# A four-layer decoder trunk on one core: attention steps only after column products, and useless products in the sequence of a score

## The chip, the cores and the metric

One core of a Trainium2 chip runs the whole kernel. The metric is the device time of one execution in microseconds, and the median of several executions. The engines are TensorE (matrix products; the profile calls its products PE and its weight loads PEld), VectorE (DVE), ScalarE (ACT), GpSimd (POOL) and SyncE (SP, which issues the DMAs here).

## What is computed

The reference is a trunk of four residual layers over 256 tokens of width 1024, in fp32. Layers 0 and 3 mix tokens by dilated attention, layer 1 by a short gated convolution, layer 2 by a conformer convolution, and each layer ends in a gated ConvFFN of width 2816:

```python
for i in range(DEPTH):
    a = rms_norm(h, mix_norm_pre[i])
    m = (dilated_attention_mixer, short_conv_mixer, conformer_conv_mixer)[i % 3](a, ...)
    h = h + rms_norm(m, mix_norm_post[i])
    f = conv_ffn(rms_norm(h, ffn_norm_pre[i]), ffn_w_in[i], ffn_w_conv[i], ffn_w_out[i])
    h = h + rms_norm(f, ffn_norm_post[i])
```

The attention has three groups of 16 heads of 64 columns with windows and dilations (128, 1), (512, 4), (2048, 16). Queries and keys get a partial rotary turn. The three groups of a head are joined by the softmax of their log-sum-exp, which comes to one softmax over all three groups' scores together.

## The kernel before, in words

**Products.** Activations lie with the 1024 features on the partitions (eight blocks of 128) and the 256 tokens along the free axis. A weight arrives by DMA as fp32 (`raw`), ScalarE casts it to a high part (`whi`, L192) and VectorE subtracts that for the low part (`wlo`, L198); the activations are split likewise. `mm3` (L280 to L282) multiplies high by high, high by low and low by high. A "column" (`column`) is 128 output features of 256 tokens: 8 blocks x 3 products = 24 products of 128x256. `Stream.pump` casts weight pieces ahead of use, at most ten pieces.

**Useless products.** At the start of the ConvFFN, the short convolution and the conformer, `spread_later` (L342) makes a function that a later column calls within its products: it spreads the normalizing factor over the partitions (L324), lets ScalarE copy it, and then calls `settle` (L333), whose products nobody reads. They use 64 rows each, the lower and the upper half of the rows in turn.

**Attention (L810).** Heads go in quads of four and pairs of two. For each quad `order` (L110) gives the blocks: a and b are the first and second pair's queries and keys for a group (`qk_block`, two columns: 48 products), v the quad's values for a group (`value`, L880, two halves of 24 products, L894 to L896). The order is "a0 a1 v0 a2 v1 b0 v2 b1 b2", in the last quad "a0 a1 v0 a2 v1 b0 b1 b2 v2". The output of a `qk_block` gets its rotary turn on VectorE in halves (`one`, `two_`, for group 0 also `parts`), which stand in the list `later` and are taken one by one by `fill`.

Between the products of these blocks a generator does the rest of an earlier pair's work, one step at each call of `step()` (L981). Its steps for a pair (`pair_work`, L955) are: what is left in `later` is issued; scores of the first 128 tokens for both heads (`scores`, L902, products at L913, 64 rows each, the two heads in turn: three products of 256 columns and two of 128) and their softmax (`soften`: mask add with minimum L920, exponential L922, L924, L925 on VectorE and ScalarE); an empty step; the same for the other 128 tokens; four turns (`turn`: four transposes L931 into one bank, two copies on ScalarE L933); the weighting of the values (`weigh`, L942, then a split on ScalarE and VectorE). The first pair waits for LAG calls of `step()`. What is left after the last block stands between the output products, in pieces of 12 products.

`step()` is called in `qk_block` after each of its two columns, in `value` between its halves (L887) and once after a value block (L1015). PSUM has banks by tag: four "A" (columns, values), three "B" (scores take two, a turn one, a weighting one), one "S". A tile's bank is used again when its last reader is done.

Of the kernel before, what the change touches and what calls it, by code (L numbers as in the profile page):

```python
# [10 lines left out]
F32 = mybir.dt.float32  # L11
# [5 lines left out]
P = 128  # L17
D = 1024
T = 256
# [17 lines left out]
SPLIT = 60  # L37
FIRST = 10
EVERY = 3
LAG = 8  # L40
NCST = 2 * P + ROT // 2

PCOLS = {}
# [185 lines left out]
def trunk_kernel(ctx: ExitStack, tc: tile.TileContext, xT, pos, params, consts, masks, w8, out):  # L229
    nc = tc.nc  # L230
# [30 lines left out]
    def act(dt=F32, tag="act", bufs=NACT, shape=(P, 2, T)):  # L261
        counter[0] += 1
        return ap.tile(list(shape), dt, tag=tag, name=f"{tag}{counter[0]}", bufs=bufs)
# [11 lines left out]
    def psum(tag="A"):  # L275
        counter[0] += 1
        return ps.tile([P, 512], F32, tag=tag, name=f"ps{tag}{counter[0]}", bufs={"A": 4, "B": 3, "S": 1}[tag])
# [12 lines left out]
    def scaled(out, a, s, b=0.0):  # L290
        nc.scalar.activation(out=out, in_=a, func=AF.Identity, scale=s, bias=b)  # L291
# [28 lines left out]
    def spread(r):  # L320

        rb = psum("S")[:, :T]
        for c in range(2):
            nc.tensor.matmul(rb[:, c * P:(c + 1) * P], lhsT=r[:, c:c + 1].to_broadcast([P, P]), rhs=ident,  # L324
                             start=True, stop=True)
        return rb
# [6 lines left out]
    def settle(x, os):  # L333


        for _ in range(2):
            for half, o in enumerate(os):
                rows = slice(half * DH, (half + 1) * DH)
                nc.tensor.matmul(o, lhsT=x[0].bitcast(F32)[rows, 0:P], rhs=x[1].bitcast(F32)[rows, 0:P], start=True,
                                 stop=True, skip_group_check=True)  # L340

    def spread_later(r, x, banks):  # L342

        rb = act()[:, 0, :]

        def fill():
            o = spread(r)
            nc.scalar.copy(out=rb, in_=o)
            settle(x, [b[:, 0:P] for b in banks])

        return rb, fill

# [457 lines left out]
    def attention(l, mg, rb):  # L810
# [49 lines left out]
        def fill():  # L860
            if later:
                later.pop(0)()
            else:
                st.pump(1)
# [15 lines left out]
        def value(quad, g, hook=None):  # L880
            ws = [st.take(2 * P) for _ in range(2)]
            o = psum("A")
            at = (1, 0) if l == 0 else (0, 2)
            for c in range(2):
                if c:
                    fill()
                    step()  # L887
                oc = o[:, c * T:(c + 1) * T]
                for k in range(KD):
                    if hook and (c, k) == at:  # L890
                        hook()
                    whi, wlo, n = ws[k // 4]
                    xh, xl = [x[:, c * P:(c + 1) * P] for x in xs[k]]
                    nc.tensor.matmul(oc, lhsT=xh, rhs=whi[:, k % 4, :], start=k == 0, stop=False)  # L894
                    nc.tensor.matmul(oc, lhsT=xh, rhs=wlo[:, k % 4, :], start=False, stop=False)  # L895
                    nc.tensor.matmul(oc, lhsT=xl, rhs=whi[:, k % 4, :], start=False, stop=k == KD - 1)  # L896
            v = act()
            for c in range(2):
                scaled(v[:, c, :], o[:, c * T:(c + 1) * T], rt[0][:, c:c + 1])
            vs[quad, g] = v  # L900
# [16 lines left out]
        def soften(o, c):  # L917
            s = act()[:].rearrange("p s t -> p (s t)")
            mn, sm, rl = tiny(1), tiny(1), tiny(1)
            nc.vector.tensor_tensor_reduce(out=s, in0=o, in1=msk[:, c, :], scale=1.0, scalar=3e38,  # L920
                                           op0=ALU.add, op1=ALU.min, accum_out=mn)
            nc.scalar.activation(out=s, in_=s, func=AF.Exp, scale=-1.0, bias=mn, accum_out=sm)  # L922
            fill()
            nc.vector.reciprocal(out=rl, in_=sm)  # L924
            nc.vector.tensor_scalar(out=s, in0=s, scalar1=rl, scalar2=None, op0=ALU.mult)  # L925
            return s

        def turn(s, pt, c):
            o = psum("B")
            for b in range(4):  # L930
                nc.tensor.transpose(o[:, b * P:(b + 1) * P], s[:, b * P:(b + 1) * P], ident)  # L931
            for b in range(2):
                nc.scalar.copy(out=pt[b][:, :, c * P:(c + 1) * P],  # L933
                               in_=o[:, b * T:(b + 1) * T].rearrange("p (b t) -> p b t", b=2))
# [20 lines left out]
        def pair_work(pair):  # L955
            while later:
                later.pop(0)()
            pts = [(act(), act()) for _ in range(2)]
            ss = []
            os = scores(pair, 0)  # L960
            ss += [soften(o, 0) for o in os]
            yield
            yield
            os = scores(pair, 1)
            ss += [soften(o, 1) for o in os]
            yield
            turn(ss[0], pts[0], 0)
            yield
            turn(ss[1], pts[1], 0)
            yield  # L970
            for hp in range(2):
                turn(ss[2 + hp], pts[hp], 1)
                yield
            while (pair // 2, 2) not in vs:
                yield True
            weigh(pair, pts)
            yield
# [3 lines left out]
        def step():  # L981
            if wait[0]:
                wait[0] -= 1
                return
            for w in list(work):
                try:
                    if not next(w):
                        return
                except StopIteration:
                    work.remove(w)  # L990
# [13 lines left out]
        for quad in range(NQ):  # L1004
            for what, g in order(quad):
                if what == "v":
                    while later and quad == NQ - 1 and g == 2:
                        later.pop(0)()
                    if waiting and l == 0:
                        value(quad, g, before)  # L1010
                    else:
                        value(quad, g, ropes if waiting else None)
                        waiting = []
                    st.pump(2)
                    step()  # L1015
                    fill()
                    fill()
                    continue
                pair = 2 * quad + (what == "b")
                if pair == 0 and g < 2:  # L1020
                    waiting.append((first[g][:], (0, g)))
                else:
                    qk_block((pair, g), ropes if waiting else None)
                    waiting = []
                if g == 2:
                    work.append(pair_work(pair))
                    if pair == 0:
                        wait[0] = LAG
        ws = [st.take() for _ in range(4)]
# [15 lines left out]
        for d in range(4, KD):  # L1045
            o = column(ys, psum("B")[:, :T])
# [171 lines left out]
```

## Time and profile before

| | us |
|---|---|
| median of three executions | 1566.38 |
| lowest, highest | 1560.3, 1568.5 |
| the profiled execution | 1566.16 |
| its span, first to last instruction | 1564.3 |
| TensorE products busy | 1538.2 (98%) |
| TensorE weight loads busy | 1501.4 (96%) |
| VectorE busy | 1243.2 (79%) |
| ScalarE busy | 925.8 (59%) |
| mean granted TensorE clock | 0.995 |

All rows come from the profiled execution. Busy time is the time in which an engine has an instruction under way; products overlap in their pipeline, so the spacing of their starts tells more than their durations (a 128x256 product is listed with about 0.28 us, and the next one starts after about 0.11 us). "Idle before" is the time that an engine stood still ahead of an instruction, and the name behind the arrow is what ended it.

### The profile page before, as it was taken

How to read it: one execution, taken by the hardware profiler on the slowest of the kernel's cores; microseconds unless marked ns; L12 is line 12 of the kernel's file. 1: busy time of each engine (PE TensorE's matmuls, PEld its weight loads, DVE VectorE, ACT ScalarE, POOL GpSimd, SP SyncE). 2: the span in 40 equal slices, each digit the busy share in tenths (PEclk: the TensorE clock that was granted, in tenths of full speed). 3: DMA queues.
4: the chain of work that ended last, by engine and by line, in shares of the span. 5: the costliest groups of instructions: out<-in, count | busy, mean ns of one | idle time of the engine just before them, and what ended most of it. 6: DMA issues, size and time to landing. Idle time of an engine off the chain costs nothing.

```text
span 1564.3 us, 31521 instructions
## 1 busy us (share of the span) xinstructions
PE 1538.2 (98%) x13194; PEld 1501.4 (96%) x13194; DVE 1243.2 (79%) x2177; ACT 925.8 (59%) x1623; POOL 17.9 (1%) x51
## 2 busy tenths in 40 slices
PE   6999999999999999999999999999999999999998
PEld 6999999999999999999999999999999999999997
DVE  4997877698886779888699588896888778588783
ACT  6564645575574566656576666566546446565562
POOL 4000000000000000000000000000000000000000
PEclk9999999999999999999999999999999999999999
DMA  5663433266552644655333136553544334245540
GB/s 218 216 213 139 162 141 130 81 218 223 195 202 103 219 162 167 238 197 201 115 135 108 55 135 244 191 186 135 216 162 164 133 136 163 107 156 222 190 162 28
DMA packets 36718, 256.94 MB, mean 164 GB/s; under 512 B 4320, under 2 KB 4448, under 8 KB 5984
## 3 DMA queue, kind: packets, MB, share of 16 engines
q1 hardware_dynamic: 36288, 254.93, 45.2%
q8 instruction: 103, 1.69, 0.4%
q14 instruction: 39, 0.32, 0.1%
q10 hardware_dynamic: 288, 0.01, 0.0%
HBM read 253.87 MB, written 1.05 MB: 163 GB/s over the span
## 4 chain that ended last, share of the span: by engine, by line
PE 93%; DVE 3%; ACT 1%; POOL 1%; issue 1%; DMA 1%; DVEq 0%; ACTq 0%; POOLq 0%
PE psA L537 17%; PE psB L280 10%; PE psB L282 10%; PE psB L281 10%; PE psA L280 7%; PE psA L281 7%; PE psA L282 7%; PE psA L894 3%; PE psA L895 3%; PE psA L896 3%; PE psB L731 2%; PE psB L942 2%; PE psB L913 2%; PE psA L453 2%; PE psB L931 2%; PE psA L448 2%
## 5 line engine op out<-in xcount | busy, mean ns | idle before, releaser
L198 DVE TENSOR_TENSOR wlo<-raw,whi 128x1024 fp32r<-128x1024 f32 x480 | 580.2, 1220 | 34.6 <-ACT whi L192 33.9
L192 ACT CAST whi<-raw 128x1024 fp32r<-128x1024 f32 x480 | 491.1, 1049 | 22.8 <-DMA raw<-in_w_dram 17.2
L282 PE MATMUL psB<-act,wlo 128*128 128x256 f32 x1392 | 385.6, 277 | 0.0
L280 PE MATMUL psB<-act,whi 128*128 128x256 f32 x1392 | 385.6, 277 | 0.0
L281 PE MATMUL psB<-act,whi 128*128 128x256 f32 x1392 | 385.6, 277 | 0.0
L280 PE MATMUL psA<-act,whi 128*128 128x256 f32 x1040 | 298.6, 287 | 8.0 <-ACT whi L192 7.1
L282 PE MATMUL psA<-act,wlo 128*128 128x256 f32 x1040 | 290.0, 279 | 0.5 <-DVE wlo L198 0.5
L281 PE MATMUL psA<-act,whi 128*128 128x256 f32 x1040 | 290.1, 279 | 0.2
L537 PE MATMUL psA<-act,whi 128*128 128x256 f32 x1536 | 265.1, 277 | 0.0
L282 PEld LDWEIGHTS psB<-act,wlo 128*128 128x128 f32 x1392 | 262.5, 189 | 0.0
L281 PEld LDWEIGHTS psB<-act,whi 128*128 128x128 f32 x1392 | 261.3, 188 | 0.0
L280 PEld LDWEIGHTS psB<-act,whi 128*128 128x128 f32 x1392 | 261.3, 188 | 0.0
L537 PEld LDWEIGHTS psA<-act,whi 128*128 128x128 f32 x1536 | 231.7, 188 | 0.0
L537 PE MATMUL psA<-act,wlo 128*128 128x256 f32 x768 | 212.9, 277 | 0.0
L280 PEld LDWEIGHTS psA<-act,whi 128*128 128x128 f32 x1040 | 197.0, 189 | 13.6 <-ACT whi L192 7.1
L282 PEld LDWEIGHTS psA<-act,wlo 128*128 128x128 f32 x1040 | 196.9, 189 | 0.8 <-DVE wlo L198 0.8
L281 PEld LDWEIGHTS psA<-act,whi 128*128 128x128 f32 x1040 | 196.9, 189 | 0.6 <-DVE act L285 0.5
L291 ACT ACTIVATE tmp<-act,par 128x256 f32<-128x256 f32 x176 | 80.2, 503 | 161.7 <-DVE act L285 161.7
L288 DVE SCALAR_TENSOR_TENSOR tmp<-act,par,tmp 128x255 f32<-128x255 f32 (+1 forms) x352 | 146.6, 479 | 19.7 <-ACT tmp L291 19.7
L537 PEld LDWEIGHTS psA<-act,wlo 128*128 128x128 f32 x768 | 144.9, 189 | 0.0
L285 DVE TENSOR_TENSOR act<-psB,act 128x512 f32<-128x512 f32 (+2 forms) x94 | 58.5, 625 | 82.2 <-PE psB L282 45.3
L922 ACT ACTIVATE act<-act,tiny 128x512 f32<-128x512 f32 x64 | 46.4, 725 | 110.3 <-DVE tiny L920 110.3
(126 smaller groups left out, 2189.1 us busy)
## 6 DMA issues: line engine op xcount, KB each, us to landing
raw<-in_w_dram SPq DMA_DIRECT2D x239, 1024.0 KB, 4.8
h<-in_xT_dram SPq DMA_DIRECT2D x4, 256.0 KB, 5.0
raw<-in_w_dram SPq DMA_DIRECT2D x2, 512.0 KB, 5.5
out_dram<-h SPq DMA_DIRECT2D x4, 256.0 KB, 2.0
msk<-in_masks_dram SPq DMA_DIRECT2D x1, 512.0 KB, 9.4
par<-in_params_dram SPq DMA_DIRECT2D x1, 484.0 KB, 10.1
cst<-in_consts_dram SPq DMA_DIRECT2D x1, 132.0 KB, 5.9
par<-in_params_dram ACTq DMA_DIRECT2D x1, 4.0 KB, 2.9
```

Of the source, the lines that this page charges most:

```text
L192: self.nc.scalar.copy(out=hi, in_=raw)
L198: self.nc.vector.tensor_tensor(out=lo, in0=raw, in1=hi.bitcast(F32), op=ALU.subtract)
L280: nc.tensor.matmul(o, lhsT=whi, rhs=x[0], start=first, stop=False)
L281: nc.tensor.matmul(o, lhsT=whi, rhs=x[1], start=False, stop=False)
L282: nc.tensor.matmul(o, lhsT=wlo, rhs=x[0], start=False, stop=last)
L285: nc.vector.tensor_tensor(out=out, in0=a, in1=b, op=op)
L288: nc.vector.scalar_tensor_tensor(out=out, in0=a, scalar=s, in1=b, op0=op0, op1=op1)
L291: nc.scalar.activation(out=out, in_=a, func=AF.Identity, scale=s, bias=b)
L537: nc.tensor.matmul(o, lhsT=a, rhs=b, start=first and i == 0, stop=last and i == 2, skip_group_check=True)
L894: nc.tensor.matmul(oc, lhsT=xh, rhs=whi[:, k % 4, :], start=k == 0, stop=False)
L895: nc.tensor.matmul(oc, lhsT=xh, rhs=wlo[:, k % 4, :], start=False, stop=False)
L896: nc.tensor.matmul(oc, lhsT=xl, rhs=whi[:, k % 4, :], start=False, stop=k == KD - 1)
```

## The change

It changes three things. `settle` issues five pairs of products instead of two, of 256, 256, 256, 128 and 128 columns instead of 128 and 128 (the second operand and the output are that wide). `value` no longer calls `step()` between its halves, and the block loop no longer calls it after a value block. In `pair_work` the empty step is gone, the four turns are taken two to a step, and LAG is 6 instead of 8.

```diff
-LAG = 8
+LAG = 6
...
     def settle(x, os):
 
 
-        for _ in range(2):
+        for n in (T, T, T, P, P):
             for half, o in enumerate(os):
                 rows = slice(half * DH, (half + 1) * DH)
-                nc.tensor.matmul(o, lhsT=x[0].bitcast(F32)[rows, 0:P], rhs=x[1].bitcast(F32)[rows, 0:P], start=True,
-                                 stop=True, skip_group_check=True)
+                nc.tensor.matmul(o[:, :n], lhsT=x[0].bitcast(F32)[rows, 0:P], rhs=x[1].bitcast(F32)[rows, 0:n],
+                                 start=True, stop=True, skip_group_check=True)
...
             o = spread(r)
             nc.scalar.copy(out=rb, in_=o)
-            settle(x, [b[:, 0:P] for b in banks])
+            settle(x, banks)
...
             for c in range(2):
                 if c:
                     fill()
-                    step()
                 oc = o[:, c * T:(c + 1) * T]
...
             os = scores(pair, 0)
             ss += [soften(o, 0) for o in os]
             yield
-            yield
             os = scores(pair, 1)
             ss += [soften(o, 1) for o in os]
             yield
-            turn(ss[0], pts[0], 0)
-            yield
-            turn(ss[1], pts[1], 0)
-            yield
-            for hp in range(2):
-                turn(ss[2 + hp], pts[hp], 1)
+            for c in range(2):
+                for hp in range(2):
+                    turn(ss[2 * c + hp], pts[hp], c)
                 yield
...
                     st.pump(2)
-                    step()
                     fill()
                     fill()
                     continue
```

## Rows read from the trace of the kernel before

**Rows 1.** Busy time of each engine in three stretches: attention of layer 0, two ConvFFN.

```profile
66.00:293.00 227.00, 225.34 (x2064) 216.03 (x2062) 178.13 (x318) 127.30 (x244) 0.00 (x0) 1.00 0.44 158
911.00:1084.00 173.00, 172.45 (x1508) 171.29 (x1505) 146.35 (x238) 110.21 (x175) 0.00 (x0) 1.00 0.56 201
1378.00:1551.00 173.00, 173.00 (x1472) 172.88 (x1472) 134.49 (x219) 100.02 (x162) 0.00 (x0) 1.00 0.46 165
```

The columns are the stretch, its length, then busy us of PE, PEld, DVE, ACT and POOL, the granted clock, the share of the DMA engines and GB/s.

**Rows 2.** TensorE's groups by line and shape: busy us, mean ns, idle before.

```profile
L895 PE MATMUL psA<-wlo,act 128*128 128x256 f32 x384 | 107.6, 280 | 0.0
...
L731 PE MATMUL psB<-act,tmp 128*128 128x256 f32 x156 | 34.2, 378 | 0.0
```

**Rows 3.** TensorE in order of time, ConvFFN of layers 2 and 3: start, length, instruction.

```profile
909.92 0.60 PE L324 MATMUL psS<-cst,tiny 128*128 128x128 f32 x4
910.45 0.71 PE L339 MATMUL psB<-act 64*128 64x128 f32 x8
...
1078.84 0.50 PE L306 MATMUL psS<-cst,tmp 128*128 128x1 f32 x4
...
1377.35 0.68 PE L324 MATMUL psS<-cst,tiny 128*128 128x128 f32 x4
1377.96 0.71 PE L339 MATMUL psB<-act 64*128 64x128 f32 x8
...
1552.91 0.50 PE L306 MATMUL psS<-cst,tmp 128*128 128x1 f32 x4
```

**Rows 4.** TensorE in order of time, layer 0's attention, around scores and a turn.

```profile
152.99 0.28 PE L896 MATMUL psA<-whi,act 128*128 128x256 f32 x1
153.11 0.28 PE L894 MATMUL psA<-whi,act 128*128 128x256 f32 x1
...
159.74 0.28 PE L282 MATMUL psA<-act,wlo 128*128 128x256 f32 x1
159.85 0.28 PE L280 MATMUL psA<-act,whi 128*128 128x256 f32 x1
...
162.12 0.28 PE L282 MATMUL psA<-act,wlo 128*128 128x256 f32 x1
162.24 0.60 PE L931 MATMUL psB<-cst,act 128*128 128x128 f32 x4
...
162.80 0.28 PE L895 MATMUL psA<-wlo,act 128*128 128x256 f32 x1
```

**Rows 5.** VectorE and TensorE in order of time at layer 3's first pair.

```profile
1132.35 3.49 DVE L198 TENSOR_TENSOR wlo<-raw,whi 128x1024 fp32r<-128x1024 f32 x3
...
1133.93 0.39 PE L913 MATMUL psB<-act 64*128 64x256 f32 x2
...
1135.76 0.74 DVE L843 STREAM_SHUFFLE act<-psA 128x512 f32<-128x512 f32 x1
...
1138.32 0.69 DVE L920 CUSTOM_DVE_ANT_0 act<-psB,msk 128x512 f32<-128x512 f32 x1
```

**Rows 6.** The same at layer 0's last pair, which stands among the output products.

```profile
263.48 0.39 PE L913 MATMUL psB<-act 64*128 64x256 f32 x2
...
264.58 0.69 DVE L920 CUSTOM_DVE_ANT_0 act<-psB,msk 128x512 f32<-128x512 f32 x1 [0.15 <-PE psB L913]
...
272.89 0.49 DVE L925 TENSOR_SCALAR act<-act,tiny 128x512 f32<-128x512 f32 x1
```

**Rows 7.** The same at a weighting of layer 0 and its split on VectorE.

```profile
118.64 1.96 PE L942 MATMUL psB<-act,act 128*64 128x256 f32 x24
...
121.77 0.42 DVE L285 TENSOR_TENSOR act<-psB,act 128x256 fp32r<-128x256 f32 x1
```

**Rows 8.** What TensorE waited for, whole span: us in total, times, longest.

```profile
PE psB L913 <- DVE act L285: 1.7, 2, 0.8
...
PE psA L280 <- ACT act L437: 0.9, 2, 0.5
```

**Rows 9.** A group of the page: busy us, mean ns, idle before.

```profile
L192 ACT CAST whi<-raw 128x1024 fp32r<-128x1024 f32 x480 | 491.1, 1049 | 22.8 <-DMA raw<-in_w_dram 17.2
```

## The prediction

> **What bounds the kernel now.** I read the table of busy time by stretch first. In the attention stretch of layer 0 TensorE is busy for 225.3 of 227 us and VectorE for 178.1; in the ConvFFN of layers 2 and 3 TensorE is busy for 172.5 and 173.0 of 173 us, all at a granted clock of 1.00, which is the 2.4 GHz level [rows 1]. So TensorE is the bound nearly everywhere: a product that is added costs its full length, and a wait that is added costs its full length as long as TensorE stands in it.
>
> The second view is TensorE's instructions in order of time. Products of one shape (128x256) start at two different spacings. After the second score products of layer 0's pair 3, column products start about 0.113 us apart (159.74, 159.85); after its first ones, where value products follow, 0.118 us (152.99, 153.11) [rows 4]. Rounded starts hide the exact values; over a whole ConvFFN they show. From the start of the useless products to the first product of the closing sum it takes 1078.84 - 910.45 = 168.39 us in layer 2, and 1552.91 - 1377.96 = 174.95 us in layer 3, for the same instructions [rows 3]. That is 6.56 us, about 4.4 ns for each of some 1,480 products, so a "fast" and a "slow" spacing last until something else than a plain stream comes. What differs ahead: in layer 3 the four spreading products take 0.68 us, 0.08 more than in layer 2 (0.60), so they stood a moment waiting for their operand [rows 3]. The useless products (`settle`) evidently set the spacing most of the time, and once did not.
>
> **Useless products: what is added.** Today a call is four 64-row fp32 products of 128 columns, two row halves side by side; they leave eight records and take 0.71 us [rows 3]; there are six calls (four ConvFFN, the short convolution, the conformer). The change keeps the two 128-column pairs at the end and puts three 256-column pairs ahead. The operands are still read as fp32, so each is recorded as two passes (the eight records show it), and six more passes of 256 columns run per call, halves side by side. A 256-column fp32 pass costs 34.2 / 156 = 0.219 us in the conformer [rows 2]. So 6 calls x 6 x 0.219 = **+7.9 us**. Could it be hidden? Nothing stands beside it: TensorE is busy for 99 to 100% of what follows [rows 1], and the copy of the spread factor is issued ahead of it, so VectorE and ScalarE start no earlier or later. The ends: +3.9, if a 64-row pass needed half of that, as a 128-column transpose (0.109) is about half of it [rows 4], and +7.9; I take 7.9, since the row has the same width and type.
>
> **Useless products: what they bring.** Where score products are followed by column products the spacing is fast, even after the pair whose score products waited 0.8 us in their midst [rows 8] (I looked through all of them; [rows 4] has one). If the longer call works like them, layer 3's ConvFFN comes down to 168.39: **-6.6 us**.
>
> The Trainium skill, page "TensorE: Matmul & The Clock Gate", section "Back-to-back issue gap", speaks against this: it gives the spacing of an isolated stream from width and clock alone (N/2.4 + 2.5, 109 ns at 256 columns), so what stood before could change nothing, and the -6.6 would be left out of the sum. The trace does not agree: neither spacing is 109 ns, and two stretches of equal work at the same clock differ by 6.56 us [rows 1, 3].
>
> **Turned tiles, two to a step.** A turn takes from the last product ahead of it (162.12) to the second behind it (162.80) 0.68 us [rows 4]; less two products (0.227) and four transposes of 0.109 (0.60 less one length of 0.27, over three), some 17 ns are the cost of going in and out. 32 such steps go away: **-0.5 us**.
>
> **Spacing in the attention stages.** Steps no longer fall into a value block, but one may still come right before it, and score or turned products followed by value products gave the slow spacing [rows 4]. By the new order six of twelve value blocks of a layer still follow a score or a turn. Even if all 1,152 value products (384 a line [rows 2]) went from slow to fast, it would be 1,152 x 4.4 ns = 5.1 us. I take 0, and -5 to +3 as ends.
>
> **Steps that come closer together: new waits.** Per layer, 44 slots are left instead of 68, a pair uses five instead of eight, and its empty slot is gone. Where no value block lies between, score 1 now comes one column (24 x 0.1133 = 2.7 us) behind score 0, and the first two turns one column behind that. Three things then gate TensorE: the three banks of tag B (score 1's second bank is score 0's first, free when its mask add is done; the second turn's bank is score 1's first), the softmax itself, and VectorE's queue ahead of it (weight differences, and the rotary halves that `pair_work` flushes). The last pair of layer 0 shows the softmax with nothing in its way: the score starts at 263.48, the first mask add at 264.58 (+1.1), the fourth tile is done at 273.38, so 2.2 us a tile [rows 6]. With a queue: in layer 3's first pair three weight differences (3.49 us, 1.14 each) and two rotary halves (2.56 us, 1.28 each) stand ahead, and the mask add comes 4.4 us after the score [rows 5].
>
> By pairs, from the start of score 0:
> - Pair 0 starts two columns later (+5.4 us for TensorE), and VectorE does the last difference, one half, two more differences and three flushed halves, ending 9.2 us after today's start: mask add at +3.8 to +4. Score 1 wants its bank at +3.7 and gets it at +4.7: 1.0 waited. The third mask add follows two tiles (4.4) and a difference (1.1): done at +10.2, where the second turn comes at +8.9: 1.3. The last tile (+13.9) is then in time. 2.2 us.
> - Pair 2: VectorE meets TensorE at the weighting, whose split ends 3.5 us after its start [rows 7]; a difference and two flushed halves later the mask add is at +2.6, the third one ends at +8.8 and the second turn wants it at +8.0: 0.8 us.
> - Pairs 1, 3: a value block lies between: 0. Pairs 4, 6: value blocks empty the rotary queue ahead of them, mask add at +1.1 to +1.5: 0.
> - Pair 5 needs the rotary halves that it flushes itself, and today already waits 0.8 us for them in each layer [rows 8]. Without the column that lay between, 2.0 us: 1.2 more.
> - Pair 7 stands among the output products, which come in 1.4 us pieces: the second turn comes 1.0 us ahead of its bank, the last tile (+9.9 [rows 6]) is 1.4 us late; the wait of 0.5 behind the last weighting [rows 8] is covered by two pieces: 1.9.
>
> 6.1 us a layer, **+12.2 us** for two. The ends: 0, if VectorE were as free as in [rows 6] and the pieces fell well, and some +20: ScalarE issues the copies of the first turns behind the last exponentials and perhaps behind a weight cast of 1.05 us [rows 9], which would delay the bank of the fourth turn by about 0.9 us in four pairs of a layer (+7). I take the sum without it, because in [rows 6]'s pair the copies came right behind the exponential.
>
> Queues: score 1's mask adds move ahead of a column's weight difference on VectorE, the turns' copies ahead of a cast on ScalarE; pieces are taken well ahead of use, so I cost that at nothing. SP's and POOL's queues have no step in them, and weight loads keep their order.
>
> **The sum** against the profiled execution (1566.16 us, a span of 1564.3; the median of the runs is 1566.38, 0.2 above): 1566.2 + 7.9 - 6.6 - 0.5 + 12.2 = **1579 us**. A measurement can tell some 0.5% from no change, 7.8 us here: faster is below 1558.5, slower above 1574.2.
>
> **Rivals.**
> - Not slower: the waits do not come. Place: second turn and score 1's bank in pairs 0 and 2. It decides if the first mask add comes within about 1.8 us of the score, as in [rows 6], also there. Then 1579 - 12.2 = 1567. For it: VectorE is idle for a fifth of the stage [rows 1]. Against: the 4.4 us of [rows 5].
> - The useless products do not do what they should: one ConvFFN stays slow, 1579 + 6.6 = 1586. For it: the last four passes are the same as today's, which failed once. Against: the score products' record.
>  By the Trainium skill's formula above, the -6.6 would likewise not come.
> - ScalarE's copies gate the fourth turn as well: 1579 + 7 = 1586, to 1593 with the rival before.
> - Faster: value products lose their slow spacing and no waits come: 1567 - 5 = 1562, still within 0.5%; below 1558.5 needs the 7.9 us to be cheaper too (the low end, 3.9).
>
> **How the numbers follow.** The sum 0.44 (own range 1572 to 1584), no waits 0.24, `settle` fails 0.14, copies 0.10, faster 0.08. The first case lies above 1574.2 for nine tenths, so slower is 0.40 + 0.14 + 0.10, less 0.01 for mixtures: 0.63; same 0.24 + 0.04 + 0.01 = 0.29; faster 0.08. For 8 in 10 the range goes from the no-wait case with some of its spacing gain, 1563, to both failures short of their sum, 1590.
>
> **What would show it.** Right: `settle` at about 2.0 us a call; all four ConvFFN at 168.4 plus 1.3; waits of TensorE's score and transpose lines on VectorE's mask add of some 12 us in all, mostly in pairs 0 and 7. Wrong: one ConvFFN at 176, waits under 4 us, or longer waits on ScalarE's copies than on VectorE.

## The result, and the profile after

The changed kernel takes **1611.62 us** (median of four executions, 1608.14 to 1614.70) where the kernel before takes 1566.86 beside it (four executions, 1560.30 to 1568.50): a ratio of 1.0306, with a 95% interval of 1.0276 to 1.0335. Slower was forecast; 1579 us and a range that ended at 1590 were not enough.

The profiled execution took 1614.70 us with a span of 1612.8, which is 48.5 us more than the span before. Line numbers have moved: the score products are L912, the mask add is L919, the scaling L924, the turn L930 and its copies L932.

First the page of the changed kernel: the span, the busy time of each engine, and the shares of the chain that ended last. The last line is that of the kernel before.

```profile
span 1612.8 us, 31675 instructions
...
PE 1565.2 (97%) x13266; PEld 1521.8 (94%) x13266; DVE 1244.1 (77%) x2177; ACT 925.3 (57%) x1623; POOL 18.2 (1%) x51
...
PE 80%; DVE 11%; ACT 4%; issue 2%; DMA 1%; POOL 1%; DVEq 0%; ACTq 0%; POOLq 0%
...
PE 93%; DVE 3%; ACT 1%; POOL 1%; issue 1%; DMA 1%; DVEq 0%; ACTq 0%; POOLq 0%
```

VectorE and ScalarE have the work that they had before (1243.2 and 925.8 us), yet VectorE now stands in 11% of the chain instead of 3%. It was not given work; it is now waited for. TensorE's busy time grew by 27 us, far more than the 7.9 us of added products: some of its products follow each other more slowly.

**Useless products and ConvFFN.** TensorE in order of time, the answers to [rows 3], in layer 0 and layer 2: the spreading, the useless products, and the first product of the closing sum. Columns are start, length and instruction.

```profile
328.36 0.60 PE L324 MATMUL psS<-cst,tiny 128*128 128x128 f32 x4
328.89 2.01 PE L339 MATMUL psB<-act 64*128 64x256 f32 x20
...
505.13 0.39 PE L306 MATMUL psS<-cst,tmp 128*128 128x1 f32 x3
...
945.61 0.60 PE L324 MATMUL psS<-cst,tiny 128*128 128x128 f32 x4
946.14 2.01 PE L339 MATMUL psB<-act 64*128 64x256 f32 x20
...
1115.81 0.39 PE L306 MATMUL psS<-cst,tmp 128*128 128x1 f32 x3
```

A call takes 2.01 us instead of 0.71: 1.30 more, as forecast. From its start to the closing sum it takes 505.13 - 328.89 = 176.24 us in layer 0 and 1115.81 - 946.14 = 169.67 in layer 2. Layer 1 is like layer 0 (176.24), layer 3 like layer 2 (169.69). Before it was 168.39 in layers 0 to 2 and 174.95 in layer 3 [rows 3]. So layer 3 did get the fast spacing that the prediction hoped for, but layers 0 and 1 lost it. The spreading took 0.60 us here in layers 0 and 2 alike, so no wait tells the two apart. What does is the column ahead of the spreading. I measured spacings as means over the products of a stretch, since the rounded starts hide them: where the products ahead came 113.4 ns apart, those behind the call came 117.5 to 117.8 ns apart (three times of three, layer 0 among them), and where they came 117.5 to 117.8 ns apart, those behind came 113.3 ns apart (three of three). **The new call turns the spacing over; the old one set it fast.**

With the short convolution (75.91 to 77.19) and the conformer (86.16 to 87.82), the stretches behind the six calls grew by 7.85 + 7.85 + 1.28 - 5.26 + 1.28 + 1.66 = 14.7 us, where the prediction had 7.9 - 6.6 = 1.3.

**Attention.** From the sum of the normalization ahead of the attention (in layer 3 that of layer 2's end) to that of the one behind it, layer 0 grew from 268.13 to 286.39 us and layer 3 from 280.76 to 297.74, together 35.3 us, where the prediction had 12.2 - 0.5 = 11.7. With 14.7 that is 50.0 us; the rest of the kernel got 1.5 us shorter, which I did not follow. What TensorE waited for, whole span, us in total, times and longest (the answer to [rows 8]):

```profile
PE psB L930 <- DVE tiny L919: 9.9, 8, 2.7
...
PE psB L912 <- DVE act L285: 6.2, 4, 2.1
...
PE psB L930 <- ACT act L932: 4.0, 8, 0.7
PE psB L930 <- DVE act L924: 2.0, 2, 1.0
PE psB L912 <- DVE tiny L919: 1.6, 3, 0.6
```

These five lines are 23.7 us. The same lines of before hold 1.9: 1.7 for L913 [rows 8], and this one for the turns:

```profile
PE psB L931 <- DVE tiny L920: 0.2, 1, 0.2
```

The longest wait is in pair 0 of layer 0. TensorE and VectorE there, in order of time, from the first scores on:

```profile
72.12 0.39 PE L912 MATMUL psB<-act 64*128 64x256 f32 x2
...
76.06 0.38 PE L912 MATMUL psB<-act 64*128 64x256 f32 x1
76.35 0.68 DVE L919 CUSTOM_DVE_ANT_0 act<-psB,msk 128x512 f32<-128x512 f32 x1
...
77.09 0.38 PE L912 MATMUL psB<-act 64*128 64x256 f32 x1 [0.65 <-DVE tiny L919]
...
80.92 0.60 PE L930 MATMUL psB<-cst,act 128*128 128x128 f32 x4
81.20 2.36 DVE L198 TENSOR_TENSOR wlo<-raw,whi 128x1024 fp32r<-128x1024 f32 x2
83.48 0.68 DVE L919 CUSTOM_DVE_ANT_0 act<-psB,msk 128x512 f32<-128x512 f32 x1
84.23 0.65 PE L930 MATMUL psB<-cst,act 128*128 128x128 f32 x4 [2.71 <-DVE tiny L919]
85.42 0.28 PE L280 MATMUL psA<-act,whi 128*128 128x256 f32 x1
85.53 0.35 PE L281 MATMUL psA<-act,whi 128*128 128x256 f32 x1
...
85.89 0.42 PE L280 MATMUL psA<-act,whi 128*128 128x256 f32 x1
86.11 0.41 PE L281 MATMUL psA<-act,whi 128*128 128x256 f32 x1
```

The first mask add comes 4.2 us after the score (76.35 - 72.12), so the second scores wait. The second turn could start at 81.4, but its bank holds the second half's first scores, whose mask add stands behind two weight differences on VectorE (2.36 us from 81.20) and comes at 83.48. Then a second loss begins that the prediction did not have. The column that follows starts its products 0.11 us apart at first (85.42, 85.53) and then 0.21 to 0.22 us apart (85.89, 86.11): TensorE's clock has gone down to the 1.2 GHz level after the wait of 2.71 us. Busy time by stretch shows the granted clock (the third number from the end; the columns are those of [rows 1]). A whole ConvFFN of this kernel has 1.00 there.

```profile
84.50:89.10 4.60, 4.60 (x29) 4.60 (x28) 4.45 (x9) 4.02 (x7) 0.00 (x0) 0.63 1.00 390
221.00:225.70 4.70, 4.70 (x30) 4.42 (x26) 2.63 (x9) 2.38 (x5) 0.00 (x0) 0.64 0.01 3
1322.00:1327.80 5.80, 5.80 (x30) 5.35 (x28) 3.48 (x9) 2.56 (x5) 0.00 (x0) 0.50 0.00 0
```

The second and third stretches stand behind waits of 2.14 us in pair 5 of layers 0 and 3. In all three TensorE is listed as busy all the time: a column at the lower level looks like work. From its first product to the next step such a column took 4.43, 4.54 and 5.42 us, where a column elsewhere in these stages takes 2.8 to 3.0: some 1.6, 1.6 and 2.5 us were lost.

### The profile page after: what moved, and what is told of

Read it like the earlier page. It is cut to its first block, busy times and chain, and to the rows that moved or that the text cites. A ratio compares the mean times of both kernels' runs of the same rounds, so it can differ in the third digit from the quotient of the medians.

```text
span 1612.8 us, 31675 instructions
## 1 busy us (share of the span) xinstructions
PE 1565.2 (97%) x13266; PEld 1521.8 (94%) x13266; DVE 1244.1 (77%) x2177; ACT 925.3 (57%) x1623; POOL 18.2 (1%) x51
## 4 chain that ended last, share of the span: by engine, by line
PE 80%; DVE 11%; ACT 4%; issue 2%; DMA 1%; POOL 1%; DVEq 0%; ACTq 0%; POOLq 0%
PE psA L537 16%; PE psB L282 10%; PE psB L280 10%; PE psB L281 10%; PE psA L280 4%; PE psA L282 4%; PE psA L281 4%; DVE wlo L198 3%; DVE act L285 3%; PE psA L893 2%; PE psA L894 2%; PE psA L895 2%; PE psB L731 2%; PE psB L941 2%; PE psA L453 2%
## 5 line engine op out<-in xcount | busy, mean ns | idle before, releaser
L282 PEld LDWEIGHTS psA<-act,wlo 128*128 128x128 f32 x1040 | 200.1, 192 | 0.8 <-DVE wlo L198 0.8
L288 DVE SCALAR_TENSOR_TENSOR tmp<-act,par,tmp 128x255 f32<-128x255 f32 (+1 forms) x352 | 146.6, 478 | 19.7 <-ACT tmp L291 19.7
L537 PEld LDWEIGHTS psA<-act,wlo 128*128 128x128 f32 x768 | 145.7, 190 | 0.0
```

The source lines that it names most:

```text
L282: nc.tensor.matmul(o, lhsT=wlo, rhs=x[0], start=False, stop=last)
L288: nc.vector.scalar_tensor_tensor(out=out, in0=a, scalar=s, in1=b, op0=op0, op1=op1)
L537: nc.tensor.matmul(o, lhsT=a, rhs=b, start=first and i == 0, stop=last and i == 2, skip_group_check=True)
```

## The experiments

Twelve runs were made, of eleven kernels. Each is set against the kernel before as it was timed beside that run. Theory A was, in short, that the new call turns the spacing over and that the steps cost waits because they stand too close together; each run says what the others were. Line numbers are those of each kernel.

### The new useless products alone

The kernel before with the change's `settle` and the wider banks, and nothing else:

```diff
-        for _ in range(2):
+        for n in (T, T, T, P, P):
...
-            settle(x, [b[:, 0:P] for b in banks])
+            settle(x, banks)
```

> The kernel before with the new useless products alone (five pairs, three of them 256 columns wide); the attention steps are as before. In the changed kernel each of the six calls left the other spacing than the one that the column ahead of it had: 113.4 became 117.8 ns three times, 117.5 to 117.8 became 113.3 three times. Theory A (the longer call turns the spacing over, whatever it was): the same here in all six calls, so the ConvFFN whose column ahead is fast take 176.2 us from the call to the closing sum, those whose column ahead is slow 169.7; with two to four slow ones the time is 1573 to 1594 us, at least 7 us over the kernel before. Rival B (the changed kernel's waits in the attention stages brought the slow ConvFFN, the call itself sets the fast spacing): all four at 169.7, time 1566 to 1570 us.

Measured: 1585.28 us (1575.05 to 1591.15, four executions) against 1560.72, ratio 1.0149 (1.0104 to 1.0195). In the profiled execution the four ConvFFN took 169.69, 176.24, 176.24 and 169.69 us from call to closing sum, and the spacing turned over behind all six calls (two from fast to slow, four from slow to fast). Attention kept its length. That is theory A; with the six calls of the changed kernel it makes twelve of twelve. The executions lie 16 us apart, which would follow if the columns ahead differ between them; only one was profiled.

### The steps alone

The change with the old `settle`: LAG, the two `step()` calls, the empty step and the turns as in the change's diff.

> The changed kernel with the old useless products (two pairs of 128 columns): the change of the steps alone. Theory A (the two attention stages lost 35 us to waits, to refilling after them and to stretches at half clock, whatever the useless products are): 1596 to 1604 us, TensorE's waits in score and transpose lines some 24 us in the profile, stretches with product starts 213 ns apart. Rival B (a good part of the attention's loss comes through the spacing that the useless products leave): under 1590 us.

Measured: 1594.83 us (1592.89 to 1598.18), ratio 1.0220 (1.0205 to 1.0235): 34.1 us more, just under theory A's range and over its rival's. All four ConvFFN took 168.39. What TensorE waited for in scores and turns is that of the changed kernel:

```profile
PE psB L930 <- DVE tiny L919: 9.9, 8, 2.7
...
PE psB L912 <- DVE act L285: 6.3, 4, 2.2
...
PE psB L930 <- ACT act L932: 3.8, 8, 0.7
```

So the two parts of the change are separate: one costs in ConvFFN, the other in attention. These three lines and two smaller ones (2.7 and 2.0) are 24.7 us of the 34.1. The medians of the two runs, 24.6 and 34.1 us over before, add up to more than the 44.8 of the changed kernel: the cost of the call differs by 16 us between executions, and before's median beside the changed kernel was 6 us higher than here.

### Two turns to a step, alone

The kernel before, with the turns paired and all else as it was:

```diff
-            turn(ss[0], pts[0], 0)
-            yield
-            turn(ss[1], pts[1], 0)
-            yield
-            for hp in range(2):
-                turn(ss[2 + hp], pts[hp], 1)
+            for c in range(2):
+                for hp in range(2):
+                    turn(ss[2 * c + hp], pts[hp], c)
                 yield
```

> The kernel before with the turned tiles taken two to a step and nothing else (steps still in and after value blocks, empty step kept). The second turn needs the third bank of tag B, which is free only when score 1's first mask add is done. Theory A (that bank gates it, but the empty step leaves time): waits of 3 to 6 us in all, mostly in the two first pairs, where that mask add ended 3 us after the place of the second turn; time 1569 to 1577. Rival B (two turns in a step are what costs the changed kernel its time): 1585 us or more. Rival C (no cost): 1564 to 1568.

Measured: 1578.32 us (1576.85 to 1578.58), ratio 1.0110 (1.0093 to 1.0127), 17.6 us more: just over theory A's range, well under its first rival's. Waits:

```profile
PE psB L931 <- DVE tiny L920: 5.0, 3, 3.3
...
PE psB L931 <- ACT act L933: 3.6, 5, 1.0
```

The second turn waits for a bank that a mask add still reads (the first line), as theory A has it, but ScalarE's copies of the turns ahead gate it nearly as much (the second).

### The empty step put back into the steps

The steps alone, with one line back:

```diff
             ss += [soften(o, 0) for o in os]
             yield
+            yield
             os = scores(pair, 1)
```

> The steps of the changed kernel, old useless products, but with the empty step between the two scores put back (six steps a pair, 48 and the six of the lag for 44 places, so more is left for the output products). Theory A (the waits come from score 1 and the first two turns following score 0 too closely): TensorE's waits in score and transpose lines fall from some 24 us to under 10 and the time to 1572 to 1585. Rival B (the waits come from two turns in one step, or from the rotary halves that a pair flushes): they stay over 16 us, and the time over 1590.

Measured: 1589.76 us (1589.16 to 1591.79), ratio 1.0187 (1.0172 to 1.0203): 29 us over before, 5 less than without the line. The waits of the second scores are gone, and those of the turns are larger:

```profile
PE psB L930 <- DVE tiny L919: 10.5, 11, 2.1
...
PE psB L930 <- ACT act L932: 5.7, 6, 1.6
```

Theory A fell here. Its rival held in the waits of scores and turns (19.7 us, over 16), and the time lies just under the 1590 that it gave: with two turns to a step, giving the scores their room back mostly moves the wait.

### Useless products like a score

The kernel before with a call that has a score's widths and also a score's types: the three wide pairs read their operands as they are (fp32r, one pass), only the two narrow pairs as fp32.

```diff
-        for _ in range(2):
+        for i, n in enumerate((T, T, T, P, P)):
...
+                a, b = (x[0], x[1]) if i < 3 else (x[0].bitcast(F32), x[1].bitcast(F32))
+                nc.tensor.matmul(o[:, :n], lhsT=a[rows, 0:P], rhs=b[rows, 0:n], start=True, stop=True,
+                                 skip_group_check=True)
```

> The kernel before with useless products of the widths of the change, but read as scores are: the three pairs of 256 columns as fp32r (one pass each), the two of 128 columns as fp32. Score products that nothing waited for left the column behind them fast 119 times in 125 in six profiles, whatever stood ahead; weightings and the new useless products, which begin with 256-column fp32 passes of 209 ns, left it turned over. Theory A (what turns the spacing over are the wide fp32 passes, not the length of the call): all six calls end fast, each ConvFFN 168.6 to 168.9 us from the call to the closing sum, time 0 to 4 us over the kernel before. Rival B (any call of five pairs turns it over): slow ConvFFN of 175 us wherever the column ahead is fast, and 7 to 30 us over the kernel before.

Measured: 1561.83 us (1559.85 to 1563.06, ten executions) against 1565.83, ratio 0.9987 (0.9971 to 1.0003). TensorE in order of time, layer 0:

```profile
310.17 1.06 PE L340 MATMUL psB<-act 64*128 64x256 f32 x14
...
478.89 0.50 PE L306 MATMUL psS<-cst,tmp 128*128 128x1 f32 x4
```

Fourteen records instead of twenty, 1.06 us instead of 2.01, and 168.72 us to the closing sum. All six calls left the fast spacing, behind columns that were fast four times and slow twice. Theory A held: not the widths, but that the wide pairs were read as fp32 (two passes each) made the change's call turn the spacing over. The type, the number of passes and the length of the call change together here, and no run parts them.

### No useless products

`settle` is not called at all; its products change no output.

> The kernel before without the useless products. Theory A (the old useless products set the fast spacing, the spreading products alone keep the one that was there): each ConvFFN has the spacing of the column ahead of it, 167.7 us where that is fast and 174.3 where it is slow; time 4 us under the kernel before, plus 6.6 for each slow one, so 1557 to 1583 and spread between executions. Rival B (the useless products do nothing): all fast, 1555 to 1558 in every execution.

Measured: 1578.41 us (1572.89 to 1583.83), ratio 1.0104 (1.0062 to 1.0146). Layer 0, from the spreading to the closing sum:

```profile
310.42 0.60 PE L324 MATMUL psS<-cst,tiny 128*128 128x128 f32 x4
...
485.05 0.50 PE L306 MATMUL psS<-cst,tmp 128*128 128x1 f32 x4
```

174.64 us, and the same in all four; from the spreading on it was 168.92 in layers 0 to 2 of before. Behind the spreading the spacing was 117.8 ns whatever it had been ahead. This is the longest of the four executions; what made two others 10 us shorter was not seen. So, in the profiled execution, part of theory A fell (the spreading does not keep what was there, it leaves slow), and part held: it is the old call that brings the fast spacing.

### No empty step, alone

The kernel before without the empty step of `pair_work`.

> The kernel before without the empty step between the two scores, nothing else. Theory A (score 1's second bank is score 0's first, free only when its mask add is done): TensorE waits in its score lines on VectorE's mask add, as the changed kernel did in pairs 0, 4 and 6, 2 to 5 us in all, and the first turns follow their softmax closely; time 4 to 14 us over the kernel before. Rival B (without two turns in one step the softmax always comes in time): 0 to 2 us over.

Measured: 1588.79 us (1587.17 to 1590.71), ratio 1.0171 (1.0145 to 1.0197). Waits of the second scores (the first line) and of first scores (the second, in pairs 3, 6 and 7):

```profile
PE psB L913 <- DVE tiny L920: 13.9, 4, 4.8
PE psB L913 <- DVE act L285: 8.3, 6, 2.3
```

The mechanism is theory A's, the size is not: 23.0 us over the median of before, 27 by the ratio, instead of 4 to 14. One wait alone is 4.8 us, on a first mask add. Theory A had no place for the second line: with a step fewer the scores of later pairs come sooner too, and wait for the rotary halves that they need.

### Two turns to a step, second head's turns in the spare bank

The run with paired turns, with the turns of the second head in bank S, so that they wait for no mask add:

```diff
-        def turn(s, pt, c):
-            o = psum("B")
+        def turn(s, pt, c, bank="B"):
+            o = psum(bank)
...
-                    turn(ss[2 * c + hp], pts[hp], c)
+                    turn(ss[2 * c + hp], pts[hp], c, "BS"[hp])
```

> The kernel before with two turns to a step, where the second head's turns go into the one bank of tag S, which stands unused in these stages, so that they don't need the third bank of tag B. With B banks alone the two-turn steps cost 17.6 us. Theory A (the second turn waits for score 1's first mask add to free the third bank): TensorE's waits in the transposes on the mask add fall from 5.0 us to under 1.5, the stretch at half clock at the first pair goes, and the time is 4 to 12 us over the kernel before. Rival B (the turns wait for the softmax and for ScalarE's copies anyway): 14 us or more over.

Measured: 1587.46 us (1585.28 to 1588.89), ratio 1.0165 (1.0135 to 1.0195): worse than without it. The turns' waits on the mask add are gone, as theory A had it, but the wait has moved, here in the list of waits:

```profile
PE psS L931 <- ACT act L933: 13.2, 12, 3.7
```

and ScalarE in order of time at the worst of them:

```profile
82.81 0.72 ACT L922 ACTIVATE act<-act,tiny 128x512 f32<-128x512 f32 x1 [1.61 <-DVE tiny L920]
...
83.54 1.98 ACT L192 CAST whi<-raw 128x1024 fp32r<-128x1024 f32 x2
85.42 0.63 ACT L933 COPY act<-psB 128x256 f32<-128x256 f32 x2
```

The copies that free the bank stand behind the exponential and two weight casts. My theory of the bank was not enough: the rival, ScalarE's copies, is the next gate.

### The call like a score, again

The same kernel as above, in five rounds.

> The kernel before with useless products read as scores are, timed again beside the kernel before on one chip with more executions. It costs 0.33 us more a call than the old ones, 2 us in all, and should leave every ConvFFN fast. Theory A (the old ones fail now and then, these don't): every execution between 1559 and 1564 us; against a kernel before that falls to 1566 in part of its executions the median is 0 to 4 us lower, never over 2 us higher. Rival B (they fail as often): executions at 1568 and more.

Measured: 1560.54 us (1559.48 to 1562.60, twelve executions) against 1559.51 (1558.67 to 1567.82, 23 executions), ratio 1.0002 (0.9991 to 1.0013). With the first run that is 22 executions, none above 1563.1; of the kernel before beside them 13 of 36 were above 1565. All six calls were followed by the fast spacing in this run's profile too, and the kernel is no faster on the median.

### Only the wide pairs, as fp32r

The kernel before, with a call of three 256-column pairs read as fp32r and no narrow fp32 pairs.

> The kernel before with three pairs of 256-column fp32r products as the only useless ones (0.35 us of products a call instead of 0.42), so a score without its fp32 part. Theory A (any 64-row pairs behind the spreading set the fast spacing unless they are wide fp32 passes): all six calls fast, 1557 to 1563 us. Rival B (the 128-column fp32 pairs at the end do it): ConvFFN of 174 to 175 us, 1570 us or more.

Measured: 1564.45 us (1557.04 to 1573.18, twelve executions), ratio 1.0018 (0.9995 to 1.0041). The profiled execution (1560.22) had all ConvFFN fast, at 168.8 to 168.9 us from the spreading on; others were up to 13 us longer. No theory is settled by it: without the narrow fp32 pairs the call sets the fast spacing in some executions, and what decides was not seen.

### The steps in and after the value blocks put back

The steps alone, with the two `step()` calls of `value` and the block loop again, so that there are more places for fewer steps, all closer together.

> The changed kernel's pairs (no empty step, two turns a step, lag 6) with the old useless products, but with the steps within and behind value blocks put back, as in the kernel before. Theory A (the loss comes from steps that follow each other too closely, not from their being fewer): TensorE's waits in score and transpose lines stay over 20 us and the time 25 us or more over the kernel before. Rival B (fewer places for steps are what costs): waits under 10 us, less than 12 us over.

Measured: 1600.45 us (1599.76 to 1605.42), ratio 1.0264 (1.0245 to 1.0283): 41 us over before, 6 more than without them. Waits:

```profile
PE psB L913 <- DVE act L285: 18.8, 13, 2.5
...
PE psB L913 <- DVE tiny L920: 5.1, 2, 3.1
```

So fewer places alone do not explain the loss: with the places back it is larger. What both kernels share is that a pair's steps have no spare step between them. The waits are not the same ones, though: thirteen are now for the rotary turn that the scores themselves need. No run took the places away, or changed LAG, by itself.

### The steps with a shorter softmax

The steps alone, without the reciprocal and the scaling: the weights are left unnormalized.

```diff
-            nc.vector.reciprocal(out=rl, in_=sm)
-            nc.vector.tensor_scalar(out=s, in0=s, scalar1=rl, scalar2=None, op0=ALU.mult)
```

> The changed steps with the old useless products, where the softmax leaves out the reciprocal and the scaling of the scores by it (so what is turned is not normalized). It takes some 0.65 us off VectorE's chain of about 2.2 us a tile. Theory A (TensorE waits for that chain, directly or through banks and copies that follow it): the waits in score and transpose lines fall from 24 us to under 14 and the time from 34 us over the kernel before to 12 to 25. Rival B (the waits come from the rotary queue and the order on ScalarE alone): less than 6 us change.

Measured: 1574.92 us (1573.50 to 1575.27), ratio 1.0092 (1.0076 to 1.0108): 15.4 us over before instead of 34.1. Taking some 0.6 us of a tile's work from VectorE halves the waits (12.2 us are left) and more than halves the loss. The waits for the rotary turn (the first line) are what they were, those of the turns are nearly gone:

```profile
PE psB L912 <- DVE act L285: 6.5, 4, 2.2
...
PE psB L928 <- DVE tiny L919: 2.2, 1, 2.2
```

That ties more than half of the loss to VectorE's latency between a score and its turn, as theory A had it; the rest stays with the rotary turn and the second scores (6.5 and 3.5 us of waits).

## Why the prediction was wrong

The direction was named, and so were most places of the waits. Two terms of the sum failed, one in its sign and one in its size, and together (13.5 and 24 us) they account for the 1614.7 - 1579 = 36 us between the profiled execution and the sum.

- **Useless products, what is added (+7.9).** Right. 6 calls x (2.01 - 0.71) = 7.8 us, nothing hidden.
- **Useless products, what they bring (-6.6).** This step failed: "If the longer call works like them". The prediction had written a paragraph earlier that the operands are still read as fp32 and recorded as two passes; a score's wide products are single passes, and so the call was not like them. Measured +14.7 - 7.8 = +6.9. The rival "they do not do what they should" (+6.6) had it right that a ConvFFN would stay slow, but thought of a call that fails to set the spacing; this one turns it over. The run with a score's types shows what the -6.6 would have needed. Even that kernel gains little: over eight profiles with the old call, 47 of 48 calls were followed by the fast spacing, so layer 3's 174.95 us is in the one profile that the prediction had and not in every execution, as the times of 1560 to 1568 already hinted. A step that counts on removing what one profile shows should ask how often it is there.
- **The formula against it.** By the formula that the Trainium skill, page "TensorE: Matmul & The Clock Gate", section "Back-to-back issue gap", gives for the isolated gap, the -6.6 would not come and nothing else would change. The same section says that in a real kernel weight loads and products set the spacing together, so the 109 ns was never its figure for this stream. The -6.6 did not come, but not for the formula's reason: at a granted clock of 1.00 the spacing was 113.3 or 117.8 ns for the same products, and it changed with what stood ahead of a stretch.
- **Going in and out (-0.5).** Too small to see beside the rest.
- **Value blocks' spacing (0, ends -5 to +3).** Not refuted: what waits and half-clock columns leave of the 35.3 us (below) is some 1.
- **Waits (+12.2).** Attention lost 35.3 us, so with the -0.5 the term should have been about 36. Here it is by pairs, excess over the pair's length without waits, from the starts of products. Layer 0, and layer 3 where it differs much:

| pair | predicted | measured in layer 0 |
|---|---|---|
| 0 | 2.2 | 1.0 second scores, 2.9 second turn, 1.6 column at half clock, 0.4 third and fourth turn (layer 3: 2.6 in all) |
| 1 | 0 | 0.5 |
| 2 | 0.8 | 0.6 |
| 3 | 0 | 1.6 turns |
| 4 | 0 | 0.9 second scores, 2.2 turns |
| 5 | 1.2 more | 1.3 more, and 1.6 column at half clock (layer 3: 1.6 more and 2.5) |
| 6 | 0 | 1.2 first scores, 0.7 turns |
| 7 | 1.9 | 0.9 and 1.3 turns |

Pairs 2, 5 and 7 came near what was said. Three things were missed. First, "value blocks empty the rotary queue ahead of them" (pairs 4 and 6, and the like for pair 3): VectorE's queue in order at pair 4 of layer 0 says otherwise.

```profile
193.59 1.22 DVE L198 TENSOR_TENSOR wlo<-raw,whi 128x1024 fp32r<-128x1024 f32 x1 [4.25 <-ACT whi L192]
194.74 1.41 DVE L285 TENSOR_TENSOR act<-act,act 128x512 f32<-128x512 f32 x2
196.83 0.69 DVE L285 TENSOR_TENSOR act<-act,act 128x512 fp32r<-128x512 f32 x1 [0.69 <-ACT act L437]
197.44 1.22 DVE L198 TENSOR_TENSOR wlo<-raw,whi 128x1024 fp32r<-128x1024 f32 x1
198.57 0.68 DVE L919 CUSTOM_DVE_ANT_0 act<-psB,msk 128x512 f32<-128x512 f32 x1
```

The score began at 194.50. VectorE had stood idle for 4.25 us, but in front of a weight difference that waited for ScalarE's cast; behind it, in order, stood the rotary halves, and the mask add came 4.1 us after the score, not 1.1 to 1.5. The cast came right behind ScalarE's reading of the value block's output, ahead of which ScalarE had itself stood idle for 5.26 us, until TensorE had ended that block:

```profile
191.79 0.84 ACT L291 ACTIVATE act<-psA,tiny 128x256 f32<-128x256 f32 x2 [5.26 <-PE psA L895]
...
192.51 1.99 ACT L192 CAST whi<-raw 128x1024 fp32r<-128x1024 f32 x2
```

So here the value block did not empty VectorE's queue; it held it up, and the work came in a bunch behind the block, where the scores were. An idle engine with a queue is not a free engine. Second, a wait costs more than the idle time shown: from one turn to the next it took 84.23 - 80.92 = 3.31 us, where turns that do not wait follow each other after 0.44, so 2.87 were lost and 2.71 are listed; over all score and turn steps the starts give some 29 us more than before, the waits 21.8 more. Third, the columns at half clock behind the three longest waits lost some 5.6 us (1.6, 1.6 and 2.5). With the -0.5, 29 + 5.6 - 0.5 is some 34 of the 35.3.
- **ScalarE's copies (rival, +7, chance 0.10).** They came on top: 4.0 us of waits for L932, and in the runs with paired turns they were what the wait moved to. The choice to leave them out, because copies came right behind the exponential in [rows 6]'s pair, took a pair without weight casts as the rule.
- **Not slower (rival, 0.24).** Its place was right, its condition was not met: at pair 0 the first mask add came 4.2 us after the score, not within 1.8. The sum had 3.8 to 4 there and 1.0 for the second scores, and got the second turn wrong (1.3): two weight differences stood ahead of the third mask add, not one.

## What to carry to other kernels

An empty step, or one tile to a step, in a hand-made order is slack for another engine's in-order queue; taking one away is costed with the whole queue of that engine, what its head is waiting for included, and not with its mean idle share. Here the empty step alone was worth some 23 us and the turns taken singly 17.6, though hardly a wait showed while they stood. The two are not to be added: all changes of the steps together cost 34.1. Products that exist only for what they leave behind must be copied in every property from what is known to work (type and passes, not only shape), and tried behind both states of what precedes them.

## What the runs showed of the hardware

- 128x256 products ran at two steady spacings, 113.3 and 117.8 ns, at one granted clock (1.00), and in a ConvFFN kept theirs for some 1,480 products. What stood ahead changed it. The spreading alone left it slow (six of six in the profile without useless products). The old call set it fast (47 of 48 in eight profiles), and so did the call with a score's types (twelve of twelve in two profiles). The call with wide fp32 passes turned it over (twelve of twelve). Over six profiles (the two kernels and the first four runs), scores without a wait left the next column fast 119 times of 125; scores with a wait in their midst, behind a fast column, left it slow 11 times of 16. What in the chip makes the two spacings stays open.
- The weightings, which begin with the same 256-column fp32 passes as the changed call, bear this out: in those six profiles they turned the spacing over 54 times of 64 where a column came behind them, and in none of 26 cases with a column ahead and value products behind.
- Waits of 2.71, 2.14 and 2.14 us in attention were followed, within 1.5 us of TensorE's start after them, by products 0.21 us apart, and by a granted clock of 0.63, 0.64 and 0.50 over a column's time. Behind the shorter waits of this profile's attention (up to 1.34 us) the clock stayed at 1.00. The length of a wait alone does not tell: in the run with the shorter softmax waits of 2.23 us in pair 5 of both layers, and in the run without the empty step waits of 2.27 us in pair 3 of both, were followed by a granted clock of 1.00. What decides stays open.
- The best kernel tried is that of before with the call like a score: 1560.5 to 1561.8 us in two medians, never above 1563.1 in 22 executions, and not faster than before's better executions.
